# Shorter roots, other PSUM banks for mixer B's keys and values, a later first head, and four gates evacuated by ScalarE

## The chip, the cores and the metric

The kernel runs on one core of a Trainium2 chip. Its time is the device time of one execution in microseconds (us), of which three runs are given. The profile comes from one further execution. TensorE (PE) multiplies matrices, with its weight loads (PEld) beside it; VectorE (DVE), ScalarE (ACT) and GpSimd (POOL) work on tiles in SBUF, the first two also on the banks of PSUM into which TensorE writes; SyncE (SP) issues most transfers. Each engine runs its own list of instructions in a fixed order and waits at an instruction until what it needs is there.

## The reference, cut to what matters

The input is x, 512 positions of 1024 channels in fp32, and two layers are computed. In each layer:

```
h = rms_norm(x)
z = h @ w_in          # q, k, v of mixer A; its index q, k, weights;
                      # cq (384), ckv (256), k_rope (32) of mixer B; gates ga, gb (1024 each)
# mixer A: 8 heads of 64; index scores, the 128 best keys of a query kept (top-k), softmax with bias
# mixer B: 8 heads
q  = rms_norm(rope_on_last_32(rms_norm(cq) @ w_uq))        # 96 per head
kv = rms_norm(ckv) @ w_ukv                                 # 64 key + 64 value channels per head
k  = rms_norm(concat(kv[..., :64], rope(k_rope)));  v = kv[..., 64:]
y_b = softmax(q k^T, block-causal) v
merged = sigmoid(ga + b) * (y_a @ w_a) + sigmoid(gb + b) * (y_b @ w_b)
x = x + merged @ w_out
# then norm, up-projection, causal convolution of width 3, SwiGLU, down-projection, residual
```

Every rms_norm needs 1/sqrt of a mean of squares plus 1e-6. The change concerns how these roots are computed, mixer B's preparation and the gates gb.

## The kernel before, in words

Every fp32 operand of a matmul is split into two parts of the type fp32r, a high one (names ending in h) and a low one (l), and a product takes three matmuls: high by high, high by low, low by high. Weights arrive by DMA as wr; ScalarE casts the high part wh, and VectorE or ScalarE with GpSimd makes the low part wl.

PSUM has eight banks in pools: D (two) for the large projections, L (three) for scores and mixer B's small projections, T (two) for transposes, Y (one) for the products of probabilities and values. A matmul that starts a bank waits until the bank's last reader is done.

The program is written as generators, which a feeder weaves together: while a head of a mixer is computed, each() lets pieces of projections run ahead as filler, at a rate per step. A scheduler then puts each engine's instructions in an order by its own estimate of times, so an instruction can stand far from its place in the code; later(n, f) puts f some steps off. The top-k search of mixer A's index scores (side_tk, rounds of three MAX and three MATCH_REPLACE over tiles of 512, 384 and 256 columns, L1036 and L1043, then sel at L1047) runs on VectorE alone beside the projections and mixer B.

Mixer B's preparation is done for two groups of four heads. In group g a loop over four tiles of 128 positions takes a bank of L (`p = bank(BB)`, BB = 'L'), multiplies ckv by the weights (L856, six matmuls of 512 columns), copies the key half to kn (ScalarE, L862), splits the value half into vb (ScalarE the high part, VectorE the low part, L315) and sums the keys' squares (ScalarE L843, VectorE L844). A bank is free after the last of these. Then mk at L870/L871 adds the rotary part's sum and forms the mean, rsqrt takes the root, and L880 scales kn. The queries take a bank of L as well (L893, nine matmuls of 384 columns), have their root from mq (L918) and are scaled at L924. In what follows uq1_1 is the second of group 1's four query tiles. Then TensorE transposes qn and kn (L1149), which are evacuated as tbh and tbl, scores are formed in L (L1164 to L1166), VectorE takes their maximum mx (L1167), ScalarE exponentiates into P (L369), VectorE scales P by the reciprocal sum rs (L1063), TensorE transposes P (L1074) and multiplies by the values into Y (L1081).

rsqrt makes a first guess with integer arithmetic and refines it by three Newton steps of three operations, all on VectorE (L346 and L355 to L357): ten operations, one tile after another. Norm.finish takes v, the root, and copies it to rstd (L486). The gates' projections end in D and are multiplied by the norm's row at the evacuation (evac_gate, L702, VectorE).

Of the kernel before, what the change touches and what calls it, by code (L numbers as in the profile page):

```python
# [15 lines left out]
OP = mybir.AluOpType  # L16
AX = mybir.AxisListType
# [7 lines left out]
EPS = 1e-6  # L25
# [20 lines left out]
GAP_B = 12  # L46
# [16 lines left out]
PBO = 0  # L63
# [14 lines left out]
GBL = 0  # L78
# [3 lines left out]
NEWT = 1  # L82
# [14 lines left out]
BB = 'L'  # L97
LAG_N = 16
# [148 lines left out]
def trunk(ctx: ExitStack, tc: tile.TileContext, xT, wd, vecs, bias, rot_n, outT):  # L247
# [95 lines left out]
    def rsqrt(a, shape, quick=False):  # L343

        y, t = small("y", shape), small("t", shape)
        V.tensor_scalar(y.bitcast(I32), a.bitcast(I32), -0.5, float(0x5F3759DF), op0=OP.mult, op1=OP.add)  # L346
        if not (quick or NEWT):
            for _ in range(3):
                G.tensor_tensor(out=t, in0=y, in1=y, op=OP.mult)
                G.tensor_tensor(out=t, in0=t, in1=a, op=OP.mult)  # L350
                G.tensor_scalar(t, t, -0.5, 1.5, op0=OP.mult, op1=OP.add)
                G.tensor_tensor(out=y, in0=y, in1=t, op=OP.mult)
            return y
        for _ in range(3):
            V.tensor_tensor(out=t, in0=y, in1=y, op=OP.mult)  # L355
            V.scalar_tensor_tensor(t, t, -0.5, a, op0=OP.mult, op1=OP.mult)
            V.scalar_tensor_tensor(y, t, 1.5, y, op0=OP.add, op1=OP.mult)  # L357
        return y
# [92 lines left out]
    class Norm:  # L451
# [17 lines left out]
        def finish(self, gap, turned):  # L469
# [15 lines left out]
            r = rsqrt(v, [4], quick=True)  # L485
            V.tensor_copy(self.rstd, r)  # L486
# [81 lines left out]
    st = {}  # L568
# [3 lines left out]
    def mix_dense(l, nrm):  # L572
# [23 lines left out]
        def turn_wk(wk):  # L596
# [36 lines left out]
            later(6, lambda: V.tensor_reduce(out=ss, in_=t3, axis=AX.X, op=OP.add))  # L633
# [62 lines left out]
        def evac_gate(name, m, p):  # L696
            g = slot(name)
            if name == "gb" and GBL and not PBO:
                A.copy(g, p)
                late.append((g, nrm.row))  # L700
            else:
                tables["v"] = V.tensor_tensor(out=g, in0=p, in1=nrm.row, op=OP.mult)  # L702
            st[name][m] = g
# [129 lines left out]
        def attn_b(g):  # L833
# [15 lines left out]
            for t in range(4):  # L849
                ts = slice(t * 128, (t + 1) * 128)  # L850
                p = bank(BB)
# [16 lines left out]
            def keys():  # L868
                m = small("mk", [4, 4])
                V.tensor_tensor(out=m, in0=ssk, in1=st["sskr"][:, :, None].to_broadcast([128, 4, 4]), op=OP.add)  # L870
                V.tensor_scalar(m, m, 1.0 / 96, EPS, op0=OP.mult, op1=OP.add)  # L871
# [360 lines left out]
    for l in range(DEPTH):  # L1232
# [33 lines left out]
        def mixer(name, scores, turn, v, each, group):  # L1266
# [6 lines left out]
            for h in range(8):  # L1273
# [3 lines left out]
                each.at(h)  # L1277
                if turn:
# [32 lines left out]
        for g, row in late:  # L1311
            V.tensor_tensor(out=g, in0=g, in1=row, op=OP.mult)
        late.clear()
# [337 lines left out]
```

## Time and profile before

| | us |
|---|---|
| median of 3 runs | 1536.77 |
| lowest and highest | 1535.88, 1537.10 |
| the profiled execution | 1536.24 |
| its span | 1534.5 |
| TensorE busy in it | 1525.7 |
| VectorE busy | 1124.4 |
| ScalarE busy | 946.3 |
| GpSimd busy | 396.3 |

The granted clock of TensorE is 1.0 throughout. A busy time is the union of an engine's instructions; a stretch of the span names its start and end in us. In layer 0 mixer B's preparation and first head lie at about 90 to 135 us, in layer 1 at about 850 to 897. In a timeline row the columns are start, duration, engine, line, operation, result and operands with their shapes, and in brackets idle time of the engine just before it and whose end ended it. Matmuls overlap, so a matmul's price is read from start to start.

### The profile page before, as it was taken

To read this page: it belongs to the slowest core of one execution; us is meant where nothing else is said; L and a number is where in the kernel's file an instruction comes from. 1 tells how busy PE (TensorE), PEld (TensorE's weight loads), DVE (VectorE), ACT (ScalarE), POOL (GpSimd) and SP (SyncE) were. 2 spreads that over 40 slices of the span, in tenths; PEclk is the share of its full clock that TensorE was granted. 3 is DMA by queue.
4 is the path that set the end of the run, shared out by engine and by line. 5 is a ranking of instruction groups with operands and counts; after the bars stand their busy time and mean duration, and the time that the engine had idled before them with its cause. 6 is when DMAs were issued, how large, how long until landed. Compare 5 with 4: busy or idle time off the path is not lost.

```text
span 1534.5 us, 23946 instructions
## 1 busy us (share of the span) xinstructions
PE 1525.7 (99%) x8658; PEld 1335.7 (87%) x8658; DVE 1124.4 (73%) x2305; ACT 946.3 (62%) x1553; POOL 396.3 (26%) x578
## 2 busy tenths in 40 slices
PE   9999999999999999999999999999999999999999
PEld 8887999888888898889998889998888888988899
DVE  7899988666476693547979999886674857835586
ACT  7756668773577536664557576687635765456642
POOL 2343012400011442124602520223001115311364
PEclk9999999999999999999999999999999999999999
DMA  7464124733488438873454641356436783488732
GB/s 247 108 158 119 53 86 113 190 118 116 128 191 190 104 117 218 194 177 90 152 171 112 159 107 56 104 134 174 129 97 147 182 189 91 149 197 197 181 99 91
DMA packets 73575, 216.29 MB, mean 141 GB/s; under 512 B 8432, under 2 KB 11504, under 8 KB 73456
## 3 DMA queue, kind: packets, MB, share of 16 engines
q1 hardware_dynamic: 54592, 149.08, 30.7%
q0 software_dynamic: 18432, 65.28, 22.8%
q8 instruction: 68, 1.11, 0.3%
q14 instruction: 51, 0.42, 0.1%
q10 hardware_dynamic: 432, 0.40, 0.1%
HBM read 141.06 MB, written 4.19 MB: 95 GB/s over the span
## 4 chain that ended last, share of the span: by engine, by line
PE 86%; DVE 11%; ACT 2%; issue 1%; DMA 0%; SPq 0%; DVEq 0%; ACTq 0%
PE D L535 37%; PE T L535 15%; PE D L558 7%; PE L L1446 5%; PE T L1446 4%; PE D L1446 3%; DVE sc L1043 2%; PE Y L1081 2%; DVE m L1036 2%; PE Y L1446 2%; PE T L1074 2%; PE L L535 2%; PE L L336 1%; PE L L335 1%; PE L L728 1%
## 5 line engine op out<-in xcount | busy, mean ns | idle before, releaser
L182 ACT CAST wh<-wr 128x1024 fp32r<-128x1024 f32 (+2 forms) x205 | 211.3, 1034 | 163.7 <-PE D L535 73.8
L211 POOL DMA_DIRECT2D wl<-wr x128 | 110.7, 874 | 630.2 <-ACT wl L210 591.9
L535 PE MATMUL D<-hxh,wh 128*128 128x512 f32 (+1 forms) x440 | 174.0, 396 | 0.0
L535 PE MATMUL D<-hxl,wh 128*128 128x512 f32 (+1 forms) x440 | 172.8, 393 | 0.0
L210 ACT ACTIVATE wl<-wr 128x1024 fp32r<-128x1024 f32 (+2 forms) x128 | 132.2, 1035 | 48.1 <-PE D L535 25.9
L200 ACT CAST wh<-wr 128x896 fp32r<-128x896 f32 x88 | 82.6, 942 | 102.4 <-POOL wr L224 56.2
L1115 POOL TENSOR_TENSOR P<-M,sel 128x128 f32<-128x128 f32 (+1 forms) x64 | 53.4, 889 | 271.2 <-DMA M<-in_bias_dram 150.2
L535 PE MATMUL D<-hxh,wl 128*128 128x512 f32 (+1 forms) x440 | 117.8, 393 | 0.0
L224 POOL TENSOR_TENSOR wr<-wr 128x256 f32<-128x256 f32 x88 | 101.0, 1151 | 57.9 <-DVE wr L223 41.9
L558 PE MATMUL D<-wh,hxh 128*128 128x256 f32 x384 | 113.8, 297 | 0.0
L205 DVE TENSOR_TENSOR wl<-wr,wh 128x896 fp32r<-128x896 f32 x88 | 101.9, 1161 | 10.2 <-ACT wh L200 4.3
L558 PE MATMUL D<-wl,hxh 128*128 128x256 f32 x384 | 109.3, 285 | 0.0
L558 PE MATMUL D<-wh,hxl 128*128 128x256 f32 x384 | 108.4, 283 | 0.0
L535 PE MATMUL D<-hrl,wh 128*128 128x512 f32 x256 | 99.6, 389 | 0.0
L535 PE MATMUL D<-hrh,wh 128*128 128x512 f32 x256 | 99.6, 389 | 0.0
L535 PE MATMUL T<-hrh,wh 128*128 128x512 f32 x256 | 99.6, 389 | 0.0
L535 PE MATMUL T<-hrl,wh 128*128 128x512 f32 x256 | 99.6, 389 | 0.0
L194 DVE TENSOR_TENSOR wl<-wr,wh 128x1024 fp32r<-128x1024 f32 x77 | 94.9, 1238 | 6.3 <-ACT wh L182 5.6
L535 PEld LDWEIGHTS D<-hxh,wh 128*128 128x128 f32 x440 | 82.9, 188 | 13.4 <-DVE gb L702 0.2
L535 PEld LDWEIGHTS D<-hxl,wh 128*128 128x128 f32 x440 | 82.9, 188 | 12.7
L535 PEld LDWEIGHTS D<-hxh,wl 128*128 128x128 f32 x440 | 80.2, 188 | 14.0
L1390 DVE SCALAR_TENSOR_TENSOR c<-T,vec,c 128x511 f32<-128x511 f32 x32 | 23.9, 748 | 89.1 <-ACT c L1387 89.1
(458 smaller groups left out, 4571.4 us busy)
## 6 DMA issues: line engine op xcount, KB each, us to landing
wr<-in_wd_dram SPq DMA_DIRECT2D x197, 512.0 KB, 3.8
wl<-wr POOLq DMA_DIRECT2D x120, 512.0 KB, 5.4
wr<-in_wd_dram SPq DMA_DIRECT2D x88, 256.0 KB, 2.6
x<-in_xT_dram SPq DMA_DIRECT2D x16, 256.0 KB, 5.2
M<-in_bias_dram SPq DMA_DIRECT2D x16, 256.0 KB, 4.0
wr<-in_wd_dram SPq DMA_DIRECT2D x7, 384.0 KB, 3.2
kah<-kah SPq DMA_DIRECT2D x16, 128.0 KB, 4.3
kal<-kal SPq DMA_DIRECT2D x16, 128.0 KB, 3.8
```

Of the source, the lines that this page charges most:

```text
L182: ins = self.nc.scalar.copy(h[:, :n], t[:, :n])
L194: eng.tensor_tensor(out=o[:, c], in0=t[:, c], in1=h[:, c].bitcast(F32), op=OP.subtract)
L200: self.nc.scalar.copy(h[:, :896], t[:, 128:1024])
L205: self.later(lag, lambda: self.nc.vector.tensor_tensor(out=o[:, :896], in0=t[:, 128:1024], in1=h[:, :896].bitcast(F32), op=OP.subtract))
L210: self.nc.scalar.activation(o, t, AF.Copy, scale=-1.0)
L211: self.nc.gpsimd.dma_start(o.bitcast(F32), t, accum_op=OP.add)
L224: g(2)(out=b[:, 6:8], in0=b[:, 0:3:2], in1=b[:, 3:6:2], op=OP.add)
L535: mm(p[:, t0:], lhsT=w, rhs=x[:, t0:], start=n == 0, stop=n == len(seq) - 1, skip_group_check=True)
L558: mm(pp[b][:, t, :], lhsT=x, rhs=w, start=n == 0 and half == 0 and t == 0, stop=n == 11 and half == 1, skip_group_check=True)
L1036: ins = V.max(out=m8[i], in_=st["sc"][i][:, :128 * (i + 1)])
L1115: G.tensor_tensor(out=P[:, P0[i]:P0[i] + w], in0=M[:, 512 - w:512], in1=sel[:, SEL0[i]:SEL0[i] + w], op=OP.add)
L1446: mm(p, lhsT=w, rhs=x, start=b0, stop=b1, skip_group_check=True)
```

## The change

The roots: one Newton step of three operations, then a step of third order in four, and the last one can write straight into a given tile (out). That is eight operations with the guess, and the copy into rstd goes. The order has 22 roots on VectorE, and 2211 rows before against 2159 now.

The keys: the mean and epsilon of the rotary part are formed once a layer on GpSimd (key_sums), so that mk is one operation, not two. The banks of the key and value tiles of group 0 are L, Y, T, T and of group 1 Y, T, L, L; the queries stay in L.

The first head: GAP_B is 16, so the feeder is called 16 times, not 12, before mixer B.

The gates: gb tiles 0 to 3 are copied from D by ScalarE, and multiplied by the row later, written at heads 4 to 7 of mixer A. Tiles 4 to 7 are as before.

```
-GAP_B = 12
+GAP_B = 16
-GBL = 0
+GBL = 4
+LATE_H = (4, 5, 6, 7)
+CUBE = 0.375 ** 0.5
+KV_BANKS = ('LYTT', 'YTLL')
 ...
-    def rsqrt(a, shape, quick=False):
+    def rsqrt(a, shape, out=None):
         y, t = small("y", shape), small("t", shape)
         V.tensor_scalar(y.bitcast(I32), a.bitcast(I32), -0.5, float(0x5F3759DF), op0=OP.mult, op1=OP.add)
 ...
-        for _ in range(3):
-            V.tensor_tensor(out=t, in0=y, in1=y, op=OP.mult)
-            V.scalar_tensor_tensor(t, t, -0.5, a, op0=OP.mult, op1=OP.mult)
-            V.scalar_tensor_tensor(y, t, 1.5, y, op0=OP.add, op1=OP.mult)
-        return y
+        V.tensor_tensor(out=t, in0=y, in1=y, op=OP.mult)
+        V.scalar_tensor_tensor(t, t, -0.5, a, op0=OP.mult, op1=OP.mult)
+        V.scalar_tensor_tensor(y, t, 1.5, y, op0=OP.add, op1=OP.mult)
+        V.tensor_tensor(out=t, in0=y, in1=y, op=OP.mult)
+        V.scalar_tensor_tensor(t, t, -CUBE, a, op0=OP.mult, op1=OP.mult)
+        V.scalar_tensor_tensor(t, t, 1.25 / CUBE, t, op0=OP.add, op1=OP.mult)
+        V.scalar_tensor_tensor(y if out is None else out, t, 1.875, y, op0=OP.add, op1=OP.mult)
+        return y if out is None else out
 ...
-            r = rsqrt(v, [4], quick=True)
-            V.tensor_copy(self.rstd, r)
+            rsqrt(v, [4], self.rstd)
 ...
-            later(6, lambda: V.tensor_reduce(out=ss, in_=t3, axis=AX.X, op=OP.add))
+            def key_sums():
+                V.tensor_reduce(out=ss, in_=t3, axis=AX.X, op=OP.add)
+                G.tensor_scalar(ss, ss, 1.0 / 96, EPS, op0=OP.mult, op1=OP.add)
+            later(6, key_sums)
 ...
-            if name == "gb" and GBL and not PBO:
+            if name == "gb" and m < GBL:
                 A.copy(g, p)
                 late.append((g, nrm.row))
 ...
-                p = bank(BB)
+                p = bank(KV_BANKS[g][t])
 ...
-                V.tensor_tensor(out=m, in0=ssk, in1=st["sskr"][:, :, None].to_broadcast([128, 4, 4]), op=OP.add)
-                V.tensor_scalar(m, m, 1.0 / 96, EPS, op0=OP.mult, op1=OP.add)
+                V.scalar_tensor_tensor(m, ssk, 1.0 / 96, st["sskr"][:, :, None].to_broadcast([128, 4, 4]),
+                                       op0=OP.mult, op1=OP.add)
 ...
+                if not turn and h in LATE_H:
+                    g, row = late.pop(0)
+                    V.tensor_tensor(out=g, in0=g, in1=row, op=OP.mult)
```

The change moves instructions, and the scheduler decides where they end up. On VectorE at the first vb of layer 0, before (sc are the tiles of index scores under the top-k search, m their eight largest):

```order
L1036 MAX m_165_875<-sc_558 128x8
L702 TENSOR_TENSOR gb_1050<-D_1011,row_440 128x512
L1036 MAX m_164_874<-sc_645 128x8
L1036 MAX m_163_873<-sc_752 128x8
L1043 MATCH_REPLACE sc_558<-m_165_875,sc_558 128x512
L315 TENSOR_TENSOR vb_1061<-L_1067,vb_1061 128x4x64
```

and now:

```order
L1044 MATCH_REPLACE sc_748<-m_163_869,sc_748 128x256
L1037 MAX m_165_871<-sc_555 128x8
L1037 MAX m_164_870<-sc_643 128x8
L1037 MAX m_163_869<-sc_748 128x8
L1044 MATCH_REPLACE sc_555<-m_165_871,sc_555 128x512
L317 TENSOR_TENSOR vb_1057<-L_1063,vb_1057 128x4x64
```

The gate is gone from the row, and ahead of this vb 58 operations of the search stand where 52 did.

On TensorE at group 1's second query tile, before, with what is waited for:

```order
L856 MATMUL L_1327<-wh_1043,ckvh_788 128x512 [waits DVE_49]
L856 MATMUL L_1327<-wh_1043,ckvl_789 128x512
L856 MATMUL L_1327<-wl_1044,ckvh_788 128x512
L856 MATMUL L_1327<-wh_1043,ckvh_792 128x512
L856 MATMUL L_1327<-wh_1043,ckvl_793 128x512
L856 MATMUL L_1327<-wl_1044,ckvh_792 128x512
L893 MATMUL L_1347<-wh_1120,cqh_684 128x384 [waits DVE_49]
```

and now (L_1361 is uq1_1, whose bank held the third key and value tile of the group, L_1304):

```order
L894 MATMUL L_1338<-wl_1117,cqh_774 128x384
L894 MATMUL L_1338<-wl_1226,cqh_865 128x384 [waits DMASW1_49]
L894 MATMUL L_1361<-wh_1116,cqh_680 128x384 [waits DVE_49]
L894 MATMUL L_1361<-wh_1116,cql_681 128x384
L894 MATMUL L_1361<-wh_1116,cqh_774 128x384
L894 MATMUL L_1361<-wh_1116,cql_775 128x384
```

The key and value tiles waited for VectorE at their fourth tile; now the first wait for VectorE on a bank of L in this group is uq1_1's.

On VectorE behind the end of the top-k search of layer 0, now:

```order
L1048 TENSOR_SCALAR sel<-sc_748 128x256
L1281 TENSOR_TENSOR gb_912<-gb_912,row_437 128x512
L1100 TENSOR_TENSOR ysum_2038<-Y_1900,ylow_2037 64x512
L1168 TENSOR_REDUCE mx_2049<-L_2050 128x1
L1281 TENSOR_TENSOR gb_962<-gb_962,row_437 128x512
L1281 TENSOR_TENSOR gb_1004<-gb_1004,row_437 128x512
L1281 TENSOR_TENSOR gb_1046<-gb_1046,row_437 128x512
L196 TENSOR_TENSOR wl_2063<-wr_1710,wh_2062 128x1024
L317 TENSOR_TENSOR tbl_2075<-T_2069,tbh_2074 100x512
```

The four late multiplies stand in mixer B, at about its fourth head, and not among mixer A's heads, where the code has them.

More of the change, by code (lines that the diff above doesn't have):

```diff
@@ L81 @@
 WMOD = 1
-NEWT = 1
+CUBE = 0.375 ** 0.5
 WB = [4, 4, 3]
@@ L341, in mm3 @@
         mm(p, lhsT=al, rhs=bh, start=False, stop=stop, skip_group_check=True)
-    def rsqrt(a, shape, quick=False):
+    def rsqrt(a, shape, out=None):
         y, t = small("y", shape), small("t", shape)
         V.tensor_scalar(y.bitcast(I32), a.bitcast(I32), -0.5, float(0x5F3759DF), op0=OP.mult, op1=OP.add)
-        if not (quick or NEWT):
-            for _ in range(3):
[L349 to L352, printed above, removed]
-            return y
-        for _ in range(3):
-            V.tensor_tensor(out=t, in0=y, in1=y, op=OP.mult)
-            V.scalar_tensor_tensor(t, t, -0.5, a, op0=OP.mult, op1=OP.mult)
-            V.scalar_tensor_tensor(y, t, 1.5, y, op0=OP.add, op1=OP.mult)
-        return y
+        V.tensor_tensor(out=t, in0=y, in1=y, op=OP.mult)
[6 more added lines that the diff above has]
+        return y if out is None else out
     def pin(ins, i, k):
@@ L1310, in trunk @@
         gb = st["gb"]
-        for g, row in late:
-            V.tensor_tensor(out=g, in0=g, in1=row, op=OP.mult)
-        late.clear()
         for m in range(0 if PBO else 8):
```

## The prediction, made blind

> **What bounds the kernel now.** I read the page's first part, then the busy times by stretch, then TensorE's waits, then the timelines of TensorE (PE) and VectorE (DVE) where the waits lie.
>
> ```profile
> span 1534.5 us, 23946 instructions
> PE 1525.7 (99%) x8658; PEld 1335.7 (87%) x8658; DVE 1124.4 (73%) x2305; ACT 946.3 (62%) x1553; POOL 396.3 (26%) x578
> ```
>
> TensorE leaves 8.8 us of the span idle. The order of both kernels has the same matmuls, and the clock is 1.00 everywhere below, so a gain can come only from waits of TensorE.
>
> ```profile
> 95.00:115.00 20.00, 18.95 (x93) 16.11 (x92) 20.00 (x72) 15.02 (x35) 14.50 (x45) 1.00 0.71 177
> 115.00:135.00 20.00, 19.23 (x104) 14.80 (x103) 19.74 (x65) 14.64 (x31) 12.55 (x30) 1.00 0.52 124
> 135.00:160.00 25.00, 24.84 (x144) 21.05 (x143) 24.84 (x55) 16.65 (x41) 0.00 (x0) 1.00 0.26 85
> 857.00:877.00 20.00, 19.57 (x96) 16.73 (x94) 20.00 (x73) 16.17 (x39) 13.94 (x43) 1.00 0.76 184
> 877.00:897.00 20.00, 19.43 (x106) 15.51 (x106) 20.00 (x67) 15.43 (x30) 13.01 (x32) 1.00 0.58 126
> ```
>
> The columns are start and end, length, then busy time (and instructions) of PE, PEld, DVE, ACT, POOL, the clock, DMA share and GB/s. In mixer B's preparation and first head VectorE is busy for the whole of nearly every stretch, and there TensorE idles 1.05 + 0.77 us in layer 0 and 0.43 + 0.57 us in layer 1. Who ended the idle times:
>
> ```profile
> PE L L856 <- DVE vb L315: 1.2, 3, 0.6
> PE L L1164 <- ACT P L369: 0.6, 1, 0.6
> PE L L893 <- DVE vb L315: 0.5, 1, 0.5
> PE T L1074 <- DVE P L1063: 0.4, 1, 0.4
> ```
>
> Three of the four (columns: us in total, times, longest) end on VectorE, and the two on vb are a PSUM bank of L that the vb subtraction still reads. The L1164 wait is ScalarE's exponent, which itself needs VectorE's mx.
>
> The stalls in layer 0 are worth more than their idle time, because a matmul behind a wait also starts slowly:
>
> ```profile
> 90.27 0.39 PE L856 MATMUL L<-wh,ckvh 128*128 128x512 f32 x1
> ...
> 94.12 0.39 PE L856 MATMUL L<-wl,ckvh 128*128 128x512 f32 x1
> 94.72 0.50 PE L856 MATMUL L<-wh,ckvh 128*128 128x512 f32 x1 [0.21 <-DVE vb L315]
> ...
> 99.04 0.68 PE L893 MATMUL L<-wl,cqh 128*128 128x384 f32 x3
> 100.19 0.44 PE L893 MATMUL L<-wh,cqh 128*128 128x384 f32 x1 [0.46 <-DVE vb L315]
> ...
> 107.96 0.39 PE L535 MATMUL D<-hxl,wh 128*128 128x512 f32 x1
> 108.94 0.50 PE L856 MATMUL L<-wh,ckvh 128*128 128x512 f32 x1 [0.59 <-DVE vb L315]
> ...
> 112.01 0.33 PE L893 MATMUL L<-wh,cqh 128*128 128x384 f32 x1
> ...
> 113.05 0.68 PE L893 MATMUL L<-wl,cqh 128*128 128x384 f32 x3
> ...
> 131.83 0.39 PE L535 MATMUL D<-hxl,wh 128*128 128x512 f32 x1
> 132.78 0.50 PE L1164 MATMUL L<-tbh,tbh 100*128 100x512 f32 x1 [0.57 <-ACT P L369]
> ...
> 133.68 0.63 PE L1074 MATMUL T<-ident,P 128*128 128x128 f32 x4
> ```
>
> Seventeen 512-column matmuls lie between the starts 90.27 and 94.12, so one takes 0.227 us; six of 384 columns between 112.01 and 113.05, so 0.173. By these prices the three stalls before 112.01 cost 0.37 + 0.63 + 0.75 = 1.75 us, and the one at 132.78 costs 0.72 (131.83 + 0.227 would have been the start). The matmuls from 90.27 to the first transposes of P at 133.68 are 38.65 us by such prices; the 43.41 us that passed hold 4.76 us lost, of which 1.75 + 0.72 are the four stalls and 2.3 are many small ones.
>
> **The change, part by part.** VectorE's prices, from start to start of neighbouring rows:
>
> ```profile
> 73.44 1.46 DVE L1036 MAX8 m<-sc 128x8 f32<-128x512 f32 x3
> 74.83 0.67 DVE L702 TENSOR_TENSOR gb<-D,row 128x512 f32<-128x512 f32 x1
> 75.41 0.07 DVE L1043 MATCH_VALUE_LOAD sc<-m,sc 128x8 f32 x1
> ...
> 75.81 0.07 DVE L1043 MATCH_VALUE_LOAD sc<-m,sc 128x8 f32 x1
> ...
> 76.47 0.41 DVE L1036 MAX8 m<-sc 128x8 f32<-128x256 f32 x1
> ...
> 107.39 0.15 DVE L356 SCALAR_TENSOR_TENSOR t<-t,mk 128x16 f32<-128x16 f32 x1
> 107.47 0.55 DVE L1036 MAX8 m<-sc 128x8 f32<-128x384 f32 x1
> ...
> 110.79 0.41 DVE L315 TENSOR_TENSOR vb<-L,vb 128x256 fp32r<-128x256 f32 x1
> ```
>
> Three MAX take 1.39, a gate 0.58, a 256-wide replacement with its load 0.40 (75.41 to 75.81), a 512-wide one 0.66 (75.81 to 76.47), so the middle one about 0.53; a small step of a root between long operations 0.08. A 256-wide scaling of keys (kn) is taken like vb, 0.41 less the overlap of 0.09 that the gate's row shows: 0.32.
>
> *Gates and roots.* Four gates leave VectorE's queue ahead of mixer B: 4 x 0.58 = 2.32 us. But the order shows that the scheduler fills the room: a round of the top-k search comes ahead of the first vb, where 52 such operations stood and now 58. A round is 1.39 + 0.40 + 0.53 + 0.66 = 2.98 us, more than the gates gave. So what VectorE gains is counted by position, not by what was taken out.
>
> *Key banks, layer 0.* The key and value tiles no longer wait for L, so the 1.75 us go. The wait does not: the second query tile of the second group (uq1_1) takes the bank of L that the third vb of that group reads. TensorE arrives there at 112.01 - 1.75 - 2 x 0.227 (two D fillers that now stand behind) = 109.8. VectorE has ahead of that vb three replacements more (1.59), two MAX (0.93), three kn (0.96), four gates less (2.32) and eight small steps less (0.64): +0.5. The vb that started at 110.79 then ends at 110.79 + 0.5 + 0.32 = 111.6. One stall of 1.8 us in place of 1.75: no gain here. With it wait the fillers and the transposes queued behind it on TensorE.
>
> *First head, layer 0.* Up to the scaling by rs (P), VectorE has two MAX more, four gates and nine small steps less: 0.93 - 2.32 - 0.72 = -2.1 us, while TensorE has 0.7 us less work ahead of P's transposes (37.95). TensorE therefore no longer waits there or on the bank that ScalarE's exponent empties: 0.72 goes, and of the 2.3 us of small losses I let 0.5 go, since they lie in the same queue. Layer 0: 0.72 + 0.5 = 1.2 us; its ends are 0 (all of it returns as wait on the transposed tiles) and 2.5.
>
> *Layer 1.* The same steps from these rows:
>
> ```profile
> 870.50 0.39 PE L535 MATMUL D<-hxh,wh 128*128 128x512 f32 x1
> 871.33 0.50 PE L856 MATMUL L<-wh,ckvh 128*128 128x512 f32 x1 [0.43 <-DVE vb L315]
> ...
> 874.40 0.33 PE L893 MATMUL L<-wh,cqh 128*128 128x384 f32 x1
> ...
> 876.66 0.39 PE L535 MATMUL D<-hxh,wh 128*128 128x512 f32 x1
> 877.19 0.32 PE L1149 MATMUL T<-ident,qn 128*100 128x128 f32 x1
> ...
> 896.08 0.33 PE L1074 MATMUL T<-ident,P 128*128 128x128 f32 x1 [0.44 <-DVE P L1063]
> ...
> 873.22 0.41 DVE L315 TENSOR_TENSOR vb<-L,vb 128x256 fp32r<-128x256 f32 x1
> ```
>
> The stalls cost 0.60, 0.30 and 0.60 us (start less the start that the matmul prices give: 870.50 + 0.227 would be 870.73, 876.66 + 0.227 would be 876.89; the third is the idle 0.44 and the slow start behind it). TensorE now gets to uq1_1 at 874.40 - 0.60 - 0.68 (three D fillers moved behind) = 873.1; VectorE's third vb, at 873.22 before, moves by 0.93 + 0.93 + 0.96 - 2.32 - 0.64 = -0.1 and ends at 873.4: 0.3 in place of 0.60. At the query transposes VectorE is 0.1 us earlier and TensorE has 0.43 us more work in front, so 0.30 goes. At P VectorE is 3 x 0.58 + 0.72 = 2.5 us earlier, TensorE 1.8 + 0.6: 0.4 of the 0.60 stays. Gain 0.3 + 0.3 + 0.2 = 0.8; with the small losses beside them I take 1.0, ends 0 and 2.0.
>
> *The later head (12 to 16).* About three more steps of filler come ahead of mixer B's first head; it is work that would be done anyway, and its effect is in the counts above (0.43 us more before the transposes in layer 1).
>
> *Fewer waits and later heads.* TensorE's program has 14 waits less. A matmul behind one takes 0.50 where 0.39 is usual, so at most 14 x 0.11 = 1.5 us; I take a third, as most waits find their semaphore long set: 0.5. Top-k ends some 35 VectorE rows earlier, which lightens the heads after 135 us, where TensorE idles 0.16 us in 25: 0.5 for both layers together, ends 0 and 1.
>
> *The gates' multiplies.* They are written into mixer A, but stand in mixer B right behind the last sel, in place of top-k work that has moved forward: up to 3 x 0.58 in a row ahead of a weight split and a transposed tile for a head whose scores come some 100 matmuls later. I cost them at nothing; without that cover, 2.3 us a layer.
>
> *ScalarE and GpSimd.* Four copies a layer (about 0.6 us of 512 columns) fall where ScalarE idles between weight casts:
>
> ```profile
> 76.86 0.84 ACT L182 CAST wh<-wr 128x768 fp32r<-128x768 f32 x1 [2.61 <-PE D L535]
> ...
> L612 POOL TENSOR_SCALAR w<-w 128x32 f32<-128x32 f32 x2 | 0.7, 346 | 0.0
> ```
>
> The idle time covers them. GpSimd's one step on the keys' sums is 0.35 us at most, long before its use. The roots of the layers' norms are a dependent row on VectorE while TensorE has other work: nothing.
>
> The Trainium skill, SBUF — State Buffer, section Who interferes with whom, speaks against this step: a VectorE instruction with two inputs in SBUF contends with a GpSimd instruction that reads SBUF, and the loser blocks. The late multiplies have two such inputs where gates read PSUM before; where they stand, the row for 135 to 160 us shows GpSimd at 0.00, so by this rule too they cost nothing, while in mixer A they would not be sure of it; for the key sums it could add the 0.35 us twice, 0.7 at most.
>
> The sum: 1.2 + 1.0 + 0.5 + 0.5 = 3.2 us. The profiled execution took 1536.24 us (span 1534.5 and 1.7 around it), 0.5 below the median of 1536.77, so 1533.0 on its own scale and 1533.6 beside the median.
>
> **The rivals.**
>
> *The room is only refilled (no change).* VectorE stays full, and the stall at uq1_1 is followed by waits on the transposed tiles, as each loss is the distance to the same queue. For it: 20.00 of 20.00 busy, and a top-k round longer than the gates. Against: -2.1 and -2.5 us at P. Gain 0 to 1.5, about 1536.
>
> *All waits of the stage go.* If the small losses too belong to VectorE, layer 0 gives 1.2 + 1.8, layer 1 gives 1.9, and later heads and waits 2: 7 us, 1529.8. For it: VectorE is ahead by more than 2 us at P. Against: uq1_1 still reads L.
>
> *Slower: one long stall at uq1_1 that is not given back.* All work behind it on TensorE waits in order, fillers too, and the fillers that split the transposes have been moved. If VectorE gets to the third vb 1.5 us later than by my count (half a top-k round, 2.98 / 2, is enough), 1.5 us a layer are lost on top of 1.75 and 0.60 that return, and nothing is gained at P: 2 x 1.5 + 0.5 = 3.5, so 1540.3. It decides from a stall of 3.3 us in layer 0. Against: the count of rows ahead is exact. The late gates' 2.3 us a layer would give 1541.4 less the gains.
>
> *The change doesn't do what it says:* it does not lighten VectorE ahead of mixer B, and the gates are not in mixer A. The first half is the rival of no change; the second alone changes no time.
>
> **How the numbers follow.** The forecast has 0.50, refilled room 0.30, all waits gone 0.10, slower 0.10. About 0.2% (3.1 us) is what a measurement of this kernel can tell from no change, and my 3.2 lies just beyond: of the forecast's own range, 1532.0 to 1535.0, somewhat more than two thirds of its chance counts as faster, 0.36, and 0.14 as same. With the rival of all waits and a little of the refilled room's tail 0.48 is faster; same is 0.14 + 0.28 = 0.42; slower 0.10. The range leaves out half of the best case and most of the worst: 1530.6 to 1537.2.
>
> **What would show it.** Right: no stall at L856 in either layer; one at L893 at about 110 us of nearly 2 us, ended by vb, and a small one near 873; none at L1164 near 132; VectorE's P some 2 us earlier against TensorE's work. Wrong: TensorE idle beyond 1.8 us in 95 to 135 us or 1.0 in 857 to 897; a new wait on tbl behind the gates; a wait on ScalarE's wh between 72 and 92 us.

## The result: slower by 0.6%

The changed kernel takes 1545.83 us (median of 6 runs, 1544.19 to 1546.71), the kernel before 1536.51 us. The ratio is 1.006, with a 95% interval of 1.0047 to 1.0074. I forecast 1533.6 us, and my range ended at 1537.2. The rival that named the place, one long stall at uq1_1 that is not given back, had a chance of 0.10 and a time of 1540.3; the stall of more than 3.3 us from which it decides came, and the loss was larger than it had. One run of the kernel before took 8666.23 us and one of `n_rot4` below 2334.82 us; the medians count them, the ratios do not.

The page of the changed kernel's profile:

```profile
span 1544.8 us, 23902 instructions
PE 1527.7 (99%) x8658; PEld 1339.6 (87%) x8658; DVE 1125.3 (73%) x2253; ACT 949.4 (61%) x1561; POOL 386.0 (25%) x580
```

TensorE has the same 8658 matmuls, and VectorE is busy for as long as before (1124.4 us) with 52 instructions fewer. The span is 10.3 us longer, and TensorE's idle time went from 8.8 to 17.1 us. Its waits, grouped by line and by what ended them (us in total, times, longest):

```profile
PE L L894 <- DVE vb L317: 6.8, 2, 4.7
PE Y L1082 <- DVE ptl L317: 1.3, 2, 0.8
PE T L387 <- DVE warm L382: 1.3, 1, 1.3
PE T L1075 <- DVE kal L805: 1.2, 2, 0.6
PE L L1165 <- ACT P L367: 0.7, 1, 0.7
PE T L1150 <- DVE qn L925: 0.6, 3, 0.2
PE T L1150 <- DVE tbl L317: 0.6, 1, 0.6
PE T L1075 <- DVE qao L331: 0.5, 2, 0.2
PE D L555 <- DVE va L320: 0.5, 2, 0.2
```

The waits of the key and value tiles on vb are gone from the list. In their place the queries (L894) wait twice, 6.8 us in all. Below them stand waits that the kernel before had small or not at all: ptl, kal, va. By stretches (columns as in the prediction):

```profile
95.00:115.00 20.00, 15.34 (x78) 13.85 (x77) 20.00 (x63) 15.22 (x36) 14.31 (x47) 0.93 0.62 152
115.00:135.00 20.00, 19.34 (x100) 16.92 (x100) 19.18 (x61) 13.41 (x28) 10.20 (x30) 0.90 0.71 176
860.00:880.00 20.00, 18.84 (x93) 16.52 (x91) 20.00 (x63) 18.07 (x43) 13.54 (x44) 1.00 0.68 157
880.00:900.00 20.00, 17.77 (x95) 14.69 (x96) 20.00 (x66) 13.80 (x26) 13.60 (x37) 1.00 0.73 179
```

TensorE idles 4.66 us in 95 to 115 us, 5.32 in 95 to 135, where more than 1.8 was the prediction's sign of being wrong. The granted clock, 1.00 in every stretch before, is 0.93 and 0.90 there: the trace has it at 0.50 from 112.11 to 118.94 us. TensorE's timeline at that place:

```profile
108.83 0.69 PE L894 MATMUL L<-wl,cqh 128*128 128x384 f32 x3
114.18 0.69 PE L894 MATMUL L<-wh,cqh 128*128 128x384 f32 x1 [4.66 <-DVE vb L317]
114.67 0.53 PE L894 MATMUL L<-wh,cql 128*128 128x384 f32 x1
114.99 0.53 PE L894 MATMUL L<-wh,cqh 128*128 128x384 f32 x1
```

This is uq1_1. Its matmuls then start 0.32 us apart where 0.174 is usual; from 119 us on they are 0.17 to 0.19 apart again. The stall costs 4.8 us and the slow matmuls behind it another 2.3.

To compare all runs I added up what TensorE loses against a fixed price for each matmul (0.227 us for 512 columns, 0.174 for 384, 0.120 for 256), by its own work and not by the clock, in four stages. "Preparation" is 90 to 130 us of TensorE's work in layer 0 and 840 to 880 in layer 1: mixer B's tiles and first head. "Later heads" is 150 to 280 and 880 to 1000: the rest of mixer B, and mixer A's beginning.

| kernel | time, us | preparation, layer 0, 1 | later heads, layer 0, 1 |
|---|---|---|---|
| before | 1536.5 | 6.6, 5.0 | 9.1, 9.0 |
| changed | 1545.8 | 9.7, 7.2 | 12.0, 11.8 |

The four differences, 3.1 + 2.2 + 2.9 + 2.8 us, make 11.0, where the span grew by 10.3. Such a figure can shift by several tenths of a us with the price taken for the small matmuls and with the ends of the stages.

### The profile page after: what moved, and what is told of

Read it like the earlier page. It is cut to its first block, busy times and chain, and to the rows that moved or that the text cites. A ratio compares the mean times of both kernels' runs of the same rounds, so it can differ in the third digit from the quotient of the medians.

```text
span 1544.8 us, 23902 instructions
## 1 busy us (share of the span) xinstructions
PE 1527.7 (99%) x8658; PEld 1339.6 (87%) x8658; DVE 1125.3 (73%) x2253; ACT 949.4 (61%) x1561; POOL 386.0 (25%) x580
## 4 chain that ended last, share of the span: by engine, by line
PE 93%; DVE 5%; ACT 2%; issue 1%; ACTq 0%
PE D L532 41%; PE T L532 15%; PE D L555 7%; PE L L1447 5%; PE T L1447 4%; PE D L1447 3%; PE Y L1082 3%; PE Y L1447 2%; PE T L1075 2%; PE L L532 2%; PE L L894 1%; PE L L338 1%; PE L L337 1%; PE L L729 1%; PE T L1150 1%
## 5 line engine op out<-in xcount | busy, mean ns | idle before, releaser
L1116 POOL TENSOR_TENSOR P<-M,sel 128x128 f32<-128x128 f32 (+1 forms) x64 | 52.3, 871 | 292.1 <-DMA M<-in_bias_dram 136.5
L226 POOL TENSOR_TENSOR wr<-wr 128x256 f32<-128x256 f32 x88 | 91.8, 1046 | 65.5 <-DVE wr L225 57.0
L532 PEld LDWEIGHTS D<-hxh,wl 128*128 128x128 f32 x440 | 79.7, 188 | 13.2
```

Source lines behind the costliest of these rows:

```text
L226: g(2)(out=b[:, 6:8], in0=b[:, 0:3:2], in1=b[:, 3:6:2], op=OP.add)
L532: mm(p[:, t0:], lhsT=w, rhs=x[:, t0:], start=n == 0, stop=n == len(seq) - 1, skip_group_check=True)
L1116: G.tensor_tensor(out=P[:, P0[i]:P0[i] + w], in0=M[:, 512 - w:512], in1=sel[:, SEL0[i]:SEL0[i] + w], op=OP.add)
```

## The experiments

Beside each group of runs the kernel before ran on the same chip (medians 1536.97 to 1537.49), and each ratio is against those runs. Lines `...` in a code cut stand for lines left out.

### One part alone

`o_banks`, the banks alone:

```
+KV_BANKS = ('LYTT', 'YTLL')
...
-                p = bank(BB)
+                p = bank(KV_BANKS[g][t])
```

> The kernel before with only the new banks of the key and value tiles (L, Y, T, T and Y, T, L, L). Bank theory (the banks alone make the one long wait at the second query tile of group 1, uq1_1): the three waits of the key and value tiles in layer 0, 1.75 us, go, TensorE reaches uq1_1 near 109.5 us, VectorE's third vb ends near 111.1 as before; a stall of about 1.7 us there, no slow matmuls behind it, total within 1 us of before, so that the slowdown needs a second part. If the banks alone carry it, the time is over 1540. Refill theory (the top-k round that replaced the gates makes VectorE late): within 1 us of before.

1538.92 us, ratio 1.0013 (1.0004 to 1.0023). TensorE's waits:

```profile
PE L L894 <- DVE vb L316: 2.6, 2, 1.7
PE T L1150 <- DVE qn L925: 1.9, 2, 1.3
```

The three waits in layer 0 go, 1.6 us, and one of 1.7 us idle comes at uq1_1, then one of 1.3 at the query transposes. The clock stays at 1.00. The banks alone do not free TensorE: they let it run ahead of VectorE, and it waits further on. They do not make the stall of 4.7 us either.

`o_gates`, the four late gates alone:

```
-GBL = 0
+GBL = 4
+LATE_H = (4, 5, 6, 7)
...
-            if name == "gb" and GBL and not PBO:
+            if name == "gb" and m < GBL:
...
+                if not turn and h in LATE_H:
+                    g, row = late.pop(0)
+                    V.tensor_tensor(out=g, in0=g, in1=row, op=OP.mult)
...
```

> The kernel before with only the four gates copied by ScalarE and multiplied later. Refill theory: VectorE reaches its vb 0.7 us later or more, the waits on L grow by about that in both layers, total 1537.5 to 1540. Bank theory: without the new banks no long wait, within 1 us of before. If the later stages (mixer A's preparation, 185 to 300 us, where the changed kernel lost 2.7 us in layer 0 and 3 in layer 1) come from the late multiplies, some 3 to 6 us of loss show there.

1539.78 us, ratio 1.0018 (1.0008 to 1.0027). Fifty-eight top-k operations stand ahead of the first vb, as in the changed kernel. The preparation loses 6.8 and 6.9 us, more than before in layer 1 only; the later heads lose 9.3 and 9.3, nearly as before. So the late multiplies do not bring the later loss. The time lies in the range of the refill theory, and its sign is there too, though more in layer 1 than it said: the waits on vb grow, to 1.06 us at 110.15 and 1.93 at 874.36, where they were 0.59 and 0.43.

```profile
PE L L857 <- DVE vb L316: 3.8, 3, 1.9
```

`o_gap`, the later first head alone:

```
-GAP_B = 12
+GAP_B = 16
```

> The kernel before with only the later first head (16 filler steps, not 12). If the loss of the changed kernel in its later stages (2.7 us in layer 0, 3 in layer 1) comes from the shifted fillers, it shows here: 1539 to 1542. If not, within 1 us of before, with the small stalls at the first head a little shorter.

1542.22 us, ratio 1.0035 (1.0023 to 1.0048). The preparation of layer 0 gains 0.9 us (5.7 against 6.6), and the later heads lose 13.2 and 11.7 where 9.1 and 9.0 were lost. Its waits:

```profile
PE T L1074 <- DVE kal L804: 1.2, 2, 0.6
PE L L856 <- DVE vb L315: 0.9, 3, 0.4
PE T L1074 <- DVE qao L329: 0.8, 2, 0.6
PE Y L1081 <- DVE ptl L315: 0.6, 2, 0.4
```

kal, qao, ptl and va are the waits that appeared in the changed kernel too. The order shows what has moved: at TensorE's prices the projection matmuls ahead of the transposes of P of mixer B's last head are 5.4 us before and 4.6 here, and those between them and mixer A's first P are 14.0 before and 11.8 here. Three microseconds of filler have gone to the first heads, and the waits stand where it is missing.

`o_roots`, the shorter roots alone (the keys' two operations stay):

```
-    def rsqrt(a, shape, quick=False):
+    def rsqrt(a, shape, out=None):
...
-            r = rsqrt(v, [4], quick=True)
-            V.tensor_copy(self.rstd, r)
+            rsqrt(v, [4], self.rstd)
```

> The kernel before with only the roots in eight operations (the keys' two operations stay). By the prediction's prices VectorE has 0.6 to 0.9 us less ahead of the first head of a layer: 0 to 1.5 us faster. If the scheduler refills that room too, or shorter roots fall beside GpSimd's work at another point, anything within 1 us of before.

1541.82 us, ratio 1.0032 (1.002 to 1.0044): a kernel with 48 VectorE operations fewer is slower by 5 us. The preparation loses 7.9 and 7.0 us. Both of my readings allowed at most "within 1 us of before"; neither held. The next group of runs gives a part of the answer, for the preparation; the 1.6 us more that layer 1's later heads lose here stay unexplained.

### GpSimd beside VectorE

VectorE's timeline in the changed kernel, with GpSimd's at the same time:

```profile
102.69 0.55 DVE L1037 MAX8 m<-sc 128x8 f32<-128x384 f32 x1
103.16 1.39 DVE L349 TENSOR_TENSOR t<-y 128x16 f32<-128x16 f32 x1
104.47 0.54 DVE L845 TENSOR_REDUCE ssq<-sqb 128x4 f32<-128x384 f32 x1
...
108.27 1.53 DVE L881 TENSOR_TENSOR kn<-kn,y 128x256 f32<-128x256 f32 x3
...
113.72 0.41 DVE L317 TENSOR_TENSOR vb<-L,vb 128x256 fp32r<-128x256 f32 x1
```

```profile
102.80 0.31 POOL L907 TENSOR_TENSOR rot<-qn,rotn 128x64 f32<-128x64 f32 x1
...
104.20 0.31 POOL L912 TENSOR_TENSOR qn<-qn,rot 128x64 f32<-128x64 f32 x1
```

A step of a root over 16 columns takes 1.39 us, and the instruction behind it starts when GpSimd's row of six operations (the rotation of a query tile, L907 to L912, 102.80 to 104.51) is done. The three key scalings take 1.46 us from start to start where the prediction priced them at 0.96. I summed what VectorE's instructions take from start to start beyond their usual pitch: between 88 and 116 us 3.1 us in the changed kernel against 1.3 before, and every one of these instructions overlaps GpSimd. The Trainium skill, SBUF — State Buffer, section Who interferes with whom, states that a VectorE instruction with two inputs in SBUF contends with a GpSimd instruction that reads SBUF, and that the order of issue decides which of the two blocks. These rows agree: MAX, the reductions and vb, with at most one such input, keep their pitch. Two inputs are not the whole condition, though, for the first step of a root has one and is stretched too (0.36 us, and 0.16 at 112.11):

```profile
102.41 0.36 DVE L348 TENSOR_SCALAR y<-mk 128x16 int32<-128x16 int32 x1
...
112.11 0.16 DVE L348 TENSOR_SCALAR y<-mq 128x16 int32<-128x16 int32 x1
```

`x_norot` leaves out those six GpSimd operations in the changed kernel, so mixer B's queries are not rotated; VectorE, ScalarE and TensorE keep their instructions and their order row for row.

```
-                    w = small_rot()
-                    G.tensor_tensor(out=w[0], in0=x1, in1=b(sin), op=OP.mult)
-                    G.tensor_tensor(out=w[1], in0=x2, in1=b(sin), op=OP.mult)
-                    G.tensor_tensor(out=x1, in0=x1, in1=b(cos), op=OP.mult)
-                    G.tensor_tensor(out=x2, in0=x2, in1=b(cos), op=OP.mult)
-                    G.tensor_tensor(out=x1, in0=x1, in1=w[1], op=OP.subtract)
-                    G.tensor_tensor(out=x2, in0=x2, in1=w[0], op=OP.add)
```

> The changed kernel without the six GpSimd operations that rotate each of mixer B's query tiles (the rotation is left out, so this computes something else; TensorE's, VectorE's and ScalarE's instructions and their order are the same row for row). Contention theory: VectorE's two-input operations (roots, key scalings) were stretched by 3.1 us beside GpSimd between 88 and 116 us, against 1.3 in the kernel before; without most of GpSimd's work the third vb of group 1 starts near 111.7, not 113.7, the stall at uq1_1 falls from 4.8 to about 2.8 us, no slow matmuls follow it, and the time is some 4 us or more below the changed kernel's, 1540 to 1542. Refill theory (VectorE is late because of the extra top-k round, which is still there): third vb at 113.7, stall 4.8, time within 0.5 us of the changed kernel's.

1540.57 us, ratio 1.0023 (1.0013 to 1.0032), 5.3 us below the changed kernel. The same instructions of VectorE, and TensorE's stall:

```profile
102.94 0.16 DVE L349 TENSOR_TENSOR t<-y 128x16 f32<-128x16 f32 x1
...
106.82 1.53 DVE L881 TENSOR_TENSOR kn<-kn,y 128x256 f32<-128x256 f32 x3
...
111.54 0.41 DVE L317 TENSOR_TENSOR vb<-L,vb 128x256 fp32r<-128x256 f32 x1
```

```profile
112.01 0.56 PE L894 MATMUL L<-wh,cqh 128*128 128x384 f32 x1 [2.40 <-DVE vb L317]
112.36 0.53 PE L894 MATMUL L<-wh,cql 128*128 128x384 f32 x1
```

The root's step is back at 0.16 and the third vb at 111.54 (113.72 with the rotations). The key scalings keep their 1.53: GpSimd still multiplies the rotary part of the keys there. The stall falls to 2.6 us. The extra top-k round is still in the queue, so the rival, that this round makes VectorE late, explains at most what is left. One thing was not as expected: slow matmuls follow 2.4 us of idle time too, and cost 1.7 us.

`b_norot` does the same to the kernel before, again with the same order on the other engines.

> The kernel before without the six GpSimd operations that rotate each of mixer B's query tiles (the rotation is left out; the order of the other engines is the same row for row). Contention theory: the 1.3 and 1.1 us by which VectorE's operations were stretched in the two layers' preparations mostly go, the stalls on vb with them: 1.5 to 3.5 us faster than before. Rival (TensorE's stalls come from VectorE's own work): within 0.5 us of before.

1533.42 us, ratio 0.9973 (0.9962 to 0.9984), 3.9 us below before, more than I expected. The preparation loses 4.4 and 3.4 us (6.6 and 5.0 with the rotations), the stretched time of VectorE is 0.2 us in each layer, and of the waits on vb 0.7 us of 1.7 are left:

```profile
PE L L893 <- DVE vb L315: 0.5, 1, 0.5
...
PE L L856 <- DVE vb L315: 0.2, 1, 0.2
```

The gain is not a wait for the rotation's result that is gone: between 88 and 136 and between 845 and 900 us no idle time above 0.15 us of TensorE, VectorE or ScalarE ends on an instruction of GpSimd, in the kernel before or without the rotations. The stretched time that went, 1.1 and 0.9 us, is half of the 3.9; the other half is what TensorE's order makes of it, and is not taken apart here.

The collision was in the kernel before all along. The change moved instructions, and with them how much of VectorE's two-input work falls beside GpSimd: the stretched time in layer 0 is 2.3 us with the shorter roots alone, 1.9 with the banks, 0.9 with the gates.

### One part taken back

`u_banks`: the changed kernel with all key and value tiles in L.

```
-KV_BANKS = ('LYTT', 'YTLL')
+KV_BANKS = ('LLLL', 'LLLL')
```

> The changed kernel with all key and value tiles in L again. Bank theory: the one stall of 4.8 us with its slow matmuls (about 7 us together) goes, the three or four smaller ones come back as 2 to 4 us, TensorE at full clock throughout; 1540 to 1543. If the long stall isn't the banks' doing, TensorE still waits over 4 us once in 105 to 120 us.

1545.4 us, ratio 1.0053 (1.0038 to 1.0068), above what I expected. The long stall and the slow matmuls are gone, and the preparation of layer 0 loses 7.7 us in place of 9.7; layer 1's loses 7.6 in place of 7.2. So the long stall needs the banks, and taking them back is hardly worth anything.

`u_gap`: the changed kernel with the first head at its old place.

```
-GAP_B = 16
+GAP_B = 12
```

> The changed kernel with the first head at its old place (12). If the later losses (185 to 300 us and 920 to 1010 us of the profile: transposes of P behind kal and qao, banks of D behind va) come from the later head, as in the kernel before with that part alone, 2.7 us in layer 0 and 3 in layer 1 go: about 1540. The stall at uq1_1 in layer 0 stays near 4.8 us, as nothing ahead of it moved.

1543.39 us, ratio 1.0041 (1.0026 to 1.0056). The stall at uq1_1 stays at 4.8 us. The later heads lose 11.2 and 10.0 us: in layer 1 most of the loss goes, in layer 0 only 0.8 of 2.9. But 1.2 of what is left there is one wait on ScalarE's pth in mixer A, with the late starts around it, that the traces of the other kernels do not have:

```profile
303.37 0.39 PE L1082 MATMUL Y<-pth,va 128*128 128x256 f32 x1 [0.56 <-ACT pth L316]
```

Without it layer 0's later heads lose about 10.0 us, as in layer 1.

`u_gates` and `u_roots`: the changed kernel with all gates multiplied at once, and with the roots in ten operations.

```
-GBL = 4
-LATE_H = (4, 5, 6, 7)
+GBL = 0
+LATE_H = ()
```

```
-        V.tensor_tensor(out=t, in0=y, in1=y, op=OP.mult)
...
-        V.scalar_tensor_tensor(y if out is None else out, t, 1.875, y, op0=OP.add, op1=OP.mult)
+        for _ in range(3):
+            V.tensor_tensor(out=t, in0=y, in1=y, op=OP.mult)
+            V.scalar_tensor_tensor(t, t, -0.5, a, op0=OP.mult, op1=OP.mult)
+            V.scalar_tensor_tensor(y, t, 1.5, y, op0=OP.add, op1=OP.mult)
+        if out is not None:
+            V.tensor_copy(out, y)
```

> The changed kernel with all gates multiplied at their evacuation again. Refill theory: 53 top-k operations instead of 58 stand ahead of the first vb, VectorE's third vb of group 1 starts about 0.6 us earlier by its own prices (five operations of 2.3 to 2.6 us less, four gates of 2.3 and small steps back: -0.2 to -0.7), 113.0 to 113.5; the stall at uq1_1 stays over 4 us and the time within 1.5 us of the changed kernel's. Contention theory: VectorE's place against GpSimd's rotations shifts, so the stall can move by 1 to 2 us either way with the stretched time beside GpSimd, which was 3.1 us between 88 and 116 us.

> The changed kernel with the roots in ten operations again. By the prediction's prices VectorE is 0.6 to 0.9 us later ahead of the first head, so 0 to 1.5 us slower than the changed kernel. Contention theory: the sign follows how much of VectorE's two-input work then falls beside GpSimd's rotations; if the stretched time in 88 to 116 us falls below 2 us, the time is below the changed kernel's although VectorE does more.

1545.3 us (ratio 1.0052, 1.0034 to 1.007) and 1547.25 us (1.0062, 1.0046 to 1.0078). In both the third vb comes at 111.9 and 111.7 us, the stretched time is 1.8 and 1.5 us (3.1 in the changed kernel), and the stall at uq1_1 is 2.9 and 2.5 us. So `u_gates` went against the refill theory alone: the third vb is 1.8 us earlier, where the count of operations said 0.2 to 0.7. The stretched time that went is 1.3 us of it, and the 0.5 left fits the count. In `u_roots` VectorE has more to do and reaches it 2 us sooner. Both lose elsewhere: 12.5 and 12.8 us at layer 0's later heads.

`rg`: only the roots, the keys' one operation and the late gates are left of the change.

```
-GAP_B = 16
+GAP_B = 12
...
-KV_BANKS = ('LYTT', 'YTLL')
+KV_BANKS = ('LLLL', 'LLLL')
```

> The changed kernel with the banks all L and the first head at its old place, so that the roots, the keys' one operation and the late gates are left. The losses of TensorE between 150 and 280 us of its work were 9.1 us in the kernel before, 12.0 in the changed one, 11.2 in the changed one with the old first head, 9.3 and 9.4 with the gates alone and the roots alone. If roots and gates together bring what is left there (VectorE's order behind the earlier end of top-k), this kernel loses about 11 there and 1541 to 1544 in all; if it needs the banks too, about 9.3 and 1539 to 1541.

1540.67 us, ratio 1.0024 (1.0014 to 1.0033). The later heads lose 10.0 and 9.7 us, closer to the second of the two expectations.

### Other banks, another gap, a shorter rotation

`f_tytt`: the changed kernel with group 1's tiles in other banks.

```
-KV_BANKS = ('LYTT', 'YTLL')
+KV_BANKS = ('LYTT', 'TYTT')
```

> The changed kernel with group 1's key and value tiles in T, Y, T, T, none in L, so that no query tile shares a bank with a vb of its group. Bank theory: no wait of uq1_1 on vb at all; instead a wait on T for the first vb of the group, which VectorE reaches near 111: TensorE arrives there near 108, so 2 to 3 us of stall, no slow matmuls: 1540 to 1543. If what holds TensorE is VectorE's queue as a whole, the wait returns at the query transposes and the time stays within 2 us of the changed kernel's.

1547.66 us (1544.91 to 1549.36), ratio 1.0066 (1.0051 to 1.0081). uq1_1 no longer waits; the group's own first tile in T does, for 3.4 us idle, with slow matmuls behind it. The preparation of layer 0 loses 8.1 us. (The profiled execution took 1544.91 us, the shortest of the four.) The wait is VectorE's, and the banks only choose its place.

`o_gap10`: the kernel before with an earlier first head.

```
-GAP_B = 12
+GAP_B = 10
```

> The kernel before with the first head earlier (10 filler steps, not 12). If the later head costs by taking filler from the last heads of mixer B (3 us of projection matmuls moved from the last two heads' gaps to the first ones in the kernel with 16), an earlier one gives the last heads more: the losses between 185 and 300 us shrink or stay, those at the first head (115 to 135 us) grow; 1535 to 1538. If any move from the tuned order costs, it is over 1538.5.

1542.23 us, ratio 1.003 (1.0019 to 1.0042). The later heads lose 10.8 and 11.6 us: less filler early did not leave them better off. Twelve is a place between two that cost 5 us each, which is the second expectation: a move from the tuned order costs, either way. So that `o_gap` loses for want of filler at the later heads is argued from its waits, and not shown.

`n_rot4`, `nb_rot4` and `a_rot4` keep the whole computation and rotate a query tile in four GpSimd operations, with the sign and the doubled cosine in two tables built once; in the kernel before, before with the new banks, and the changed kernel.

```
...
+                    G.tensor_tensor(out=w, in0=x, in1=b(rot_s), op=OP.mult)
+                    G.tensor_tensor(out=x, in0=x, in1=b(rot_c), op=OP.mult)
+                    G.tensor_tensor(out=x[:, :, 0:16], in0=x[:, :, 0:16], in1=w[:, :, 16:32], op=OP.add)
+                    G.tensor_tensor(out=x[:, :, 16:32], in0=x[:, :, 16:32], in1=w[:, :, 0:16], op=OP.add)
```

> The kernel before with each query tile's rotation in four GpSimd operations (two 128 wide, two 64 wide) in place of six 64 wide, and two tables built once at the start; the whole result is computed and the other engines' order is the same row for row. Contention theory: leaving the rotation out gave 3.9 us; a quarter less of GpSimd's time there gives back 0.5 to 1.5 us: 1535.5 to 1536.5 beside a kernel before of 1537. Rival (only GpSimd's waits count, not how long it runs): within 0.3 us of before.

> The same with the new banks of the key and value tiles. If the banks only move the wait because VectorE is late beside GpSimd, the stall at uq1_1 falls below 1.7 us and the time to within 1 us of before; if VectorE's own queue sets it, it stays 1.5 to 2.5 us above before, as the banks alone.

> The changed kernel with the rotation in four operations. Contention theory: the stretched time in 88 to 116 us falls from 3.1 us by a quarter to a half, the stall at uq1_1 from 4.8 to 3 to 4 us, the time by 1 to 3 us to 1543 to 1545. Rival: as the changed kernel, within 0.5 us.

`n_rot4`: 1536.69 us, ratio 0.9994 (0.9985 to 1.0003), no clear change. `nb_rot4`: 1538.98, 1.0012 (1.0002 to 1.0021), as the banks alone; its stall at uq1_1 is shorter (1.39 us idle, 1.69 with the banks alone), but in its profiled execution the clock falls twice, as the last section shows, and with the banks alone it does not. `a_rot4`: 1542.39, 1.0031 (1.0019 to 1.0043), 3.4 us below the changed kernel. GpSimd's busy time in 95 to 135 us fell only from 27.1 to 25.0 in `n_rot4`, and VectorE's stretched time there did not fall (1.3 us in layer 0 as before, 2.0 in layer 1 where it was 1.1); in `a_rot4` it fell from 3.1 to 1.2 in layer 0. The cost goes by which instructions meet, not in proportion to GpSimd's time. No kernel that computes the whole result was clearly faster than the one before.

The runs by stage, worked out as in the table above:

| kernel | first head at | preparation, layer 0, 1 | later heads, layer 0, 1 |
|---|---|---|---|
| before | 12 | 6.6, 5.0 | 9.1, 9.0 |
| o_banks | 12 | 7.0, 5.6 | 9.1, 10.0 |
| o_gates | 12 | 6.8, 6.9 | 9.3, 9.3 |
| o_roots | 12 | 7.9, 7.0 | 9.4, 10.6 |
| rg | 12 | 7.4, 6.7 | 10.0, 9.7 |
| u_gap | 12 | 10.1, 7.1 | 11.2, 10.0 |
| b_norot | 12 | 4.4, 3.4 | 9.0, 8.8 |
| n_rot4 | 12 | 5.8, 5.5 | 9.0, 9.1 |
| nb_rot4 | 12 | 6.7, 6.8 | 9.3, 9.4 |
| changed | 16 | 9.7, 7.2 | 12.0, 11.8 |
| o_gap | 16 | 5.7, 5.2 | 13.2, 11.7 |
| u_banks | 16 | 7.7, 7.6 | 12.0, 12.0 |
| u_gates | 16 | 6.9, 7.4 | 12.5, 12.1 |
| u_roots | 16 | 7.6, 8.2 | 12.8, 12.6 |
| x_norot | 16 | 5.8, 5.3 | 11.8, 11.5 |
| a_rot4 | 16 | 6.3, 6.7 | 11.7, 11.3 |
| f_tytt | 16 | 8.1, 7.3 | 11.8, 11.8 |
| o_gap10 | 10 | 6.4, 6.0 | 10.8, 11.6 |

The later heads' column follows the place of the first head: 11.3 to 13.2 us in all kernels with 16, 8.8 to 10.6 in those with 12 but for one value, `u_gap`'s 11.2 with the wait on pth. The preparation's column goes with VectorE's collisions with GpSimd: it is smallest where the rotations are left out of the kernel before, and over the 18 kernels its correlation with the stretched time is about 0.9 in layer 0 and 0.7 in layer 1.

## Why the prediction was wrong

**The banks' gain** was right in size: 1.75 us forecast, 1.64 measured up to the queries of group 1.

**VectorE at uq1_1, layer 0,** is the first step that failed. I counted the rows ahead of the third vb, found +0.5 us, and put the stall at 1.8. It moved by 2.9 us, from 110.79 to 113.72; 0.3 of it was there before the preparation, 1.8 is stretched time beside GpSimd, and the 0.8 left is near the count's 0.5. The term missing was a price that depends on what GpSimd does at the same time. The rows were in front of me: a small step of a root at 1.39 us looks like the 1.26 that a mean of squares (mq) took in the kernel before. I applied the Trainium skill's rule on shared SBUF reads (SBUF — State Buffer, section Who interferes with whom) to the late gates and the key sums, and not to the roots and key scalings, which have two SBUF inputs and run beside GpSimd all the time. TensorE came 0.45 us earlier than I had it, at 109.35. Together the stall was 4.8 us.

**The clock** was not in the prediction at all: 2.3 us of slow matmuls behind the long stall. A wait can have a second price.

**The first head, layer 0,** came out in size, by luck. I forecast 1.2 us of gain from the rows after uq1_1; TensorE lost 4.1 us between 110 and 130 us of its work before and 2.8 now, about 1.2 less (the slow matmuls lie almost all in front of the 110). But the wait on ScalarE's exponent, whose 0.72 us were to go, is still there, and VectorE scales the first P later by the clock, not 2.1 us earlier (first before, then changed):

```profile
131.81 0.27 DVE L1063 TENSOR_SCALAR P<-P,rs 128x128 f32<-128x128 f32 x1
```

```profile
130.28 0.33 PE L1165 MATMUL L<-tbh,tbh 100*128 100x128 f32 x1 [0.65 <-ACT P L367]
...
132.91 0.28 DVE L1064 TENSOR_SCALAR P<-P,rs 128x128 f32<-128x128 f32 x1
```

TensorE transposes the first P at 136.5 us where it did at 133.68, so VectorE's lead is TensorE's own delay. The gain goes with the later head: `o_gap`, which has nothing else, loses 0.9 us less than the kernel before in layer 0's preparation, and `u_gap`, which has everything else, loses 10.1 us there, 0.4 more than the changed kernel.

**Layer 1's preparation** was to gain 1.0 us and lost 2.2. I put the stall at uq1_1 at 0.3; it was 2.4, for the same reason: VectorE was stretched by 2.0 us there against 1.1, in the key scalings above all (0.8 us of it).

**"It is work that would be done anyway, and its effect is in the counts above"**, of the later head, is the step that cost most: 5.7 us at the later heads of the two layers, where I had 0.5 of gain. By `u_gap`, without its wait on pth, the later head brings some 2 us of it in each layer. I counted filler only up to the first head, and did not ask which heads it was taken from.

**The fewer waits and the late gates' place**: the gates stand where the order had them, and alone they leave the later heads as they were, so their multiplies cost nothing there, as forecast. Of the 0.5 us for fewer waits nothing can be seen.

**The refill** was seen rightly in the order and costs something (`o_gates`), but it is not the main part of the long stall: `x_norot` keeps it and has the third vb 2.2 us earlier.

What stays open: why one part taken back returns so little (`u_banks`, `u_gates`), beyond that each moves the collisions again; and whether it is the missing filler, or any move from the tuned order, that costs at the later heads (`o_gap`, `o_gap10`).

## What to carry to other kernels

An operation's price holds only beside the work it was measured beside: where VectorE is the bound and GpSimd runs next to it, look for instructions with two SBUF inputs whose duration jumps (0.16 to 1.39 us here) before counting rows. Filler that is brought forward can be missing later, so follow it to the place it came from; and in an order that has been tuned, expect any move to cost until a run says otherwise. A stage that is bound by a second engine does not get faster when the first engine's waits are taken away one by one: the wait moves down the queue, merges, and a merged wait can cost the clock.

## What the runs showed of the hardware

After waits of TensorE of 2.35, 2.40, 2.70, 2.83, 3.36 and twice 4.66 us, in seven kernels, its granted clock stood at 0.50 for 3.41 or 6.83 us, and 384-column matmuls started 0.320 us apart in place of 0.174. One stretch of 3.41 us at half clock made the matmuls in it lose about 1.7 us. Length alone did not decide: 2.14, 1.93 and 1.89 us left the matmuls at their pace, but in `nb_rot4` the clock fell after 1.88 us in layer 1, and after 0.36 and 1.39 us close together in layer 0:

```profile
109.37 0.44 PE L901 MATMUL L<-wl,cqh 128*128 128x384 f32 x1 [0.36 <-DMA wl<-wr]
111.20 0.58 PE L901 MATMUL L<-wh,cqh 128*128 128x384 f32 x1 [1.39 <-DVE vb L315]
111.58 0.52 PE L901 MATMUL L<-wh,cql 128*128 128x384 f32 x1
```

In `u_gates` the matmuls ran at their pace for 1.3 us behind the wait, and slowed down only then:

```profile
112.39 0.45 PE L894 MATMUL L<-wh,cqh 128*128 128x384 f32 x1 [2.70 <-DVE vb L317]
112.67 0.34 PE L894 MATMUL L<-wh,cql 128*128 128x384 f32 x1
112.84 0.33 PE L894 MATMUL L<-wh,cqh 128*128 128x384 f32 x1
...
115.24 0.52 PE L894 MATMUL L<-wh,cqh 128*128 128x384 f32 x1
115.56 0.52 PE L894 MATMUL L<-wh,cql 128*128 128x384 f32 x1
```

What decides can be read from the times at which the clock changes. In every trace they lie a whole number of stretches of 3.413 us apart (in the changed kernel 105.81 us, 31 of them, at full clock, then 6.83, two, at half). Counted by these stretches, in the 18 traces, each one at full clock in which TensorE idled for 1.76 us or more is followed by half clock, and each one with 1.70 us or less by full clock. The two nearest to the limit, with the stretch behind each (`nb_rot4`, then `u_gates`; columns as in the prediction):

```profile
107.95:111.36 3.41, 1.65 (x8) 1.07 (x8) 3.41 (x14) 3.07 (x7) 3.41 (x12) 1.00 1.09 222
111.36:114.77 3.41, 3.41 (x11) 3.31 (x12) 3.41 (x12) 0.00 (x0) 2.73 (x7) 0.50 1.04 245
```

```profile
874.83:878.24 3.41, 1.71 (x10) 1.39 (x8) 3.41 (x11) 3.41 (x8) 3.41 (x13) 1.00 0.99 187
878.24:881.65 3.41, 2.64 (x13) 2.20 (x14) 3.41 (x14) 1.13 (x3) 2.77 (x12) 1.00 1.07 235
```

Where the stretches begin differs between executions (the first change recorded lies between 3.95 and 7.14 us), so the same wait can cost the clock in one and not in another. In `x_norot` two of ten executions had a mean clock of 1.000 and took 1538.51 and 1538.82 us, the eight at 0.999 took 1539.85 to 1542.57. In `nb_rot4` and `a_rot4` the times do not part that way, so what a stretch at half clock costs in the end is not settled.

The Trainium skill, TensorE: Matmul & The Clock Gate, section Part 1: The HAM clock gate, has the clock halved after an idle window of about 3.4 us that runs freely. The halving and the length of the window agree (0.50 for 3.41 us); that it must be idle throughout does not, since 1.76 us of idle time in it were enough.
